# A two-layer attention and long-convolution kernel: skip row by identity products, closing tiles in another pool, two groups of loads reordered

## The chip, the cores and the metric

The kernel runs on 1 core of one Trainium2 chip. The metric is the device time of an execution in microseconds (us). In the text the engines are PE (TensorE), DVE (VectorE), ACT (ScalarE), POOL (GpSimd) and SP (SyncE, which here issues nearly all transfers). L524 is line 524 of the kernel before; in the kernel after, the same statements stand at a line one to ten away.

## The reference

Inputs are 2048 latent tokens and 256 context tokens of width 1024, in fp32. Layer 0 has global attention (8 query heads, 2 key heads of width 64) beside a Hyena long convolution of order 2; layer 1 has windowed attention with a sink beside two-dimensional neighbourhood attention. The branches are gated, joined by an output projection, and added to the residual. What the change touches in the convolution: the filter taps of each order are divided by their norm, and the convolved signal gets the input times `skip` added.

```python
def bidir_long_conv(z, h_fwd, h_bwd, d_skip):
    n = z.shape[1]
    taps = jnp.concatenate([h_fwd, jnp.zeros_like(h_fwd[:1]), h_bwd[:0:-1]], axis=0)
    taps = taps * lax.rsqrt(jnp.sum(taps * taps, axis=0, keepdims=True) + EPS)
    zf = jnp.fft.rfft(z.astype(jnp.float32), n=2 * n, axis=1)
    tf = jnp.fft.rfft(taps, n=2 * n, axis=0)
    y = jnp.fft.irfft(zf * tf[None], n=2 * n, axis=1)[:, :n]
    return (y + z.astype(jnp.float32) * d_skip.astype(jnp.float32)).astype(z.dtype)
...
def hyena_branch(u, conv_w, conv_b, w1, b1, w2, b2, freq, w3, d_skip):
...
    for o in range(HYENA_ORDER):
        z = parts[o + 1] * bidir_long_conv(z, filt[:, o, 0], filt[:, o, 1], d_skip[o])
...
def even_mixer(p, p_ctx, q_norm, k_norm, conv_w, conv_b, w1, b1, w2, b2, freq, w3, d_skip, cos, sin, need_ctx):
...
    y_a = global_gqa(q, k, v, k_c, v_c)
    y_b = hyena_branch(hu, conv_w, conv_b, w1, b1, w2, b2, freq, w3, d_skip)
    y = jnp.concatenate([y_a * jax.nn.silu(ag), y_b * jax.nn.silu(hg)], axis=-1)
```

In each layer the mixer's output `y` goes through `x = x + gate[:, None] * jnp.matmul(y, w_out[layer])`. The kernel puts `d_skip` into the filter: adding `d_skip * sqrt(sum of squares + EPS)` to tap 0 ahead of the division by the norm is the same as adding `z * d_skip` to the convolution's result.

## The kernel before, in words

All of it is one core's program. Matrix products of fp32 data are made of three products of high and low parts (`mm3`, L222: `whi` by high, `whi` by low, `wlo` by high part). A weight tile of 256 KB is loaded by SP into a ring of three `wraw` tiles (L242), cast to `whi` by ACT (L243), and POOL makes `wlo` (L244).

Every engine takes its instructions in order. Which order that is, a list scheduler decides for each engine at build time, with modelled durations; only PE's order in the two attention stages is written by hand. So an edit to one stage can reorder the instructions of all engines around it. SP's queue matters most here: a DMA that must wait for its data or for its target's buffer holds up all DMAs behind it. Memory comes from pools that are opened and closed by stage; a pool that takes the memory of a closed one waits for that one's last users.

The stages in order of time: conditioning and the first loads (0 to 60 us); the filters of the Hyena convolution between layer-0 projections (to 600); context attention and context Hyena (to 790); projections, latent convolution and the first maxima (to 1174); global attention in 16 units, with Hyena steps and jobs of the output projection between (1190 to 2303); layer-1 projections of three groups of tokens (2303 to 2510, to 2800, to 3128); layer-1 attention (to 3720); the last output projection.

The parts that the change and the prediction touch:

- `filter_loads` (L405 to L446) lists the loads of the filters' constants; `filters` computes. `taps` (L486 to L531) is run for the context filters (twice, one round for each order `o`, near 115 to 150 us) and for the latent filters (near 560 to 600 us). In each round, four matmuls sum the squares of the taps into `pss` (L519), with the channel on the partitions (128x4); DVE adds EPS (L521), ACT and DVE make the reciprocal root `rc` (L118 to L124), and DVE multiplies to the norm `ssv` (L523). The first tap row `first[o]` has its 512 channels along one partition, so the norm must change its layout: SP stores it to HBM (`rD`, L524, single elements), reads it back as 1x512 (`ssq`, L526), loads the skip row (`dskip`, L528), and DVE multiplies and adds (L529, L530). Then `behind` casts the tap tile (L456) and transforms it (`pA`, L562).
- `finish` in `glob_attn` closes a unit of the attention: it loads the gate `agt`, sums the denominators (`pd`, L1003), copies them (`rec`, L1005), takes reciprocals in four quarters (L1008, DVE), multiplies by gate and values (L1011, L1012, POOL), and `finish_y` splits the result into `yhi` and `ylo` (L370, L371) and stores both to `yT` (L372, L373). All these tiles come from the attention's pool `ga`. Behind the last unit, the normalised input of layer 1 (`lnh`, L306, then `hT`, L307 and L308) and the gains of the norms (L273, scaled at L275) take memory of the closed `ga`.
- `out_jobs` makes the jobs of the output projection; `job` loads weights and two `oy` tiles (L1390) of a token tile and calls `mm3`. Pool `xo` holds its rings: `oy0` and `oy1` of two tiles each, 4 KB a partition.
- In each group of layer 1, `rows` and `cols` of `Proj` project: keys and values of the window, its queries, the neighbourhood's keys, queries and values (`ev_v`, tile `vt`, store `v1n`, L353), then the gates in two blocks of `cols`. The stores of queries and keys are `qk<-tq` (L215). In the last group `window_keys` (L1429 to L1444) loads mask, sink, banded keys `wk1` and `wk2` (L1441, L1442) and values (L1443) of layer 1's windowed attention, which first uses them at L1550.

Of the kernel before, what the change touches and what calls it, by code (L numbers as in the profile page):

```python
# [17 lines left out]
P = 128  # L18
# [22 lines left out]
def kern(ctx, tc, nc, I, C, out):  # L41
# [114 lines left out]
    fC = dr.tile([2, 4, P, 512], F32, tag="fC", name="fC")  # L156
    rD = dr.tile([4, 512], F32, tag="rD", name="rD")
    q0 = [dr.tile([8, P, min(512, 2304 - t)], F32, tag=f"q0{t}", name="q0") for t in range(0, 2304, 512)]
# [91 lines left out]
    class Proj:  # L250
# [98 lines left out]
        def ev_v(self, dst):  # L349
            def f(ps, tt):  # L350
                vt = self.rg.tile([P, 512], F32, tag="bo", name="vt", bufs=3)
                S.copy(vt, ps)
                nc.sync.dma_start(dst[tt], vt)  # L353
            return f
# [10 lines left out]

    def finish_y(sb, y, ft, t0, n, yT=yT, tags=("yhi", "ylo"), bufs=2, eng=None):

        hi = sb.tile([P, 512], F32R, tag=tags[0], name="yhi", bufs=bufs)
        lo = sb.tile([P, 512], F32R, tag=tags[1], name="ylo", bufs=bufs)
        S.copy(hi[:, :n], y)  # L370
        (eng or V).tensor_tensor(out=lo[:, :n], in0=y, in1=hi[:, :n].bitcast(F32), op=ALU.subtract)  # L371
        nc.sync.dma_start(yT[0, ft, :, t0:t0 + n], hi[:, :n].bitcast(F32))  # L372
        nc.sync.dma_start(yT[1, ft, :, t0:t0 + n], lo[:, :n].bitcast(F32))  # L373
# [12 lines left out]
    def scr(sb, nm):  # L386
        return sb.tile([P, 512], F32, tag="s", name=nm, bufs=SC)
# [17 lines left out]
    def filter_loads(sb, ztiles):  # L405
# [38 lines left out]
        D["dA"] = t = scr(sb, "dA")[:, 0:P]  # L444
        ld.append(lambda t=t: nc.sync.dma_start(t, C['dftAf']))
        return D, ld  # L446

    rc = [cp.tile([P, 2, 4], F32, tag=f"rc{i}", name=f"rc{i}") for i in range(2)]

    def filters(sb, ps, D):  # L450
        zf, w1, pc, w2, dl, dscc, w3, dsc, dA = (D[k] for k in ("zf", "w1", "pc", "w2", "dl", "dscc", "w3", "dsc", "dA"))
        def new(nm, *shape, tag=None, bufs=1, dt=F32R):
# [33 lines left out]
        def taps(nq, mm, dcol, behind, ctxt):  # L486
# [29 lines left out]
            for o in range(2):  # L516
                pt = ps.tile([P, 512], F32, tag="x", name="pss", bufs=3)
                for k in range(4):
                    T.matmul(pt[:, k:k + 1], acc[o][:, k * P:(k + 1) * P], ones[:, 0:1], start=True, stop=True)  # L519
                v = sb.tile([P, 4], F32, tag="ssv", name="ssv", bufs=2)  # L520
                V.tensor_scalar(out=v, in0=pt[:, 0:4], scalar1=EPS, scalar2=None, op0=ALU.add)  # L521
                rsqrt(sb, rc[ctxt][:, o, :], v, 4, "sst")
                V.tensor_tensor(out=v, in0=v, in1=rc[ctxt][:, o, :], op=ALU.mult)  # L523
                nc.sync.dma_start(rD[2 * ctxt + o].rearrange("(k p) -> p k", p=P), v)  # L524
                v = scr(sb, "ssq")[0:1]
                nc.sync.dma_start(v, rD[2 * ctxt + o:2 * ctxt + o + 1])  # L526
                ds_ = scr(sb, "dskip")[0:1]
                nc.sync.dma_start(ds_, I['hy_skip'][0, o:o + 1, :])  # L528
                V.tensor_tensor(out=v, in0=v, in1=ds_, op=ALU.mult)  # L529
                V.tensor_tensor(out=first[o][0:1, :], in0=first[o][0:1, :], in1=v, op=ALU.add)  # L530
                behind(o, 0, first[o])()  # L531
# [370 lines left out]

    def glob_attn(sb, ps, hooks, M0):

# [91 lines left out]
        def finish(n, yo, acc):  # L996

            qb, hp = units[n]
            gt = sb.tile([P, 512], F32, tag="agt", name="agt", bufs=1)
            nc.sync.dma_start(gt, g0[hp, :, qb * 512:qb * 512 + 512])  # L1000
            pd = ps.tile([P, 512], F32, tag="m", name="pd", bufs=3)
            for h in range(2):
                T.matmul(pd[64 * h:64 * h + 64, :], ones[:, 64:P], acc[:, h, :], start=True, stop=True)  # L1003
            rec = sb.tile([P, 512], F32, tag="rec", name="rec", bufs=1)
            S.copy(rec, pd)  # L1005

            def quarter(i):
                V.reciprocal(rec[:, i:i + 128], rec[:, i:i + 128])  # L1008

            def gate():  # L1010
                G.tensor_tensor(out=rec, in0=rec, in1=gt, op=ALU.mult)  # L1011
                G.tensor_tensor(out=yo, in0=yo, in1=rec, op=ALU.mult)  # L1012

            return [lambda i=i: quarter(i) for i in range(0, 512, 128)] + [gate, lambda: finish_y(sb, yo, hp, qb * 512, 512, bufs=1, eng=G)]

        batches = [(n, kt) for n in range(16) for kt in range(0, 18, 2)]
        nb = len(batches)
        acc, po, ended, last, pend = {}, {}, {}, None, []
        total = 16 * 41

# [8 lines left out]
        for b in range(nb + 4):  # L1029
# [23 lines left out]
            if last is not None:  # L1053
                m, ks, tiles = last
                if ks == 0:
                    po[m] = ps.tile([P, 512], F32, tag="o", name="po", bufs=1)
                for i in range(2):
                    values(m, ks + i, tiles[i], po[m])
                if ks == 16:
                    yo = sb.tile([P, 512], F32, tag="yo", name="yo", bufs=2)  # L1060
                    S.copy(yo, po.pop(m))
                    ended[b + 2] = m, yo
# [307 lines left out]
    def out_jobs(g, halves, xs=None, early=()):  # L1370
# [9 lines left out]
        def job(b, i, tt, mm):  # L1380
            c = slice(512 * b, 512 * b + 512)
            rg, xo, gl = O0["rg"], O0["xo"], O0["gl"]
            if i == 0 and w_out.get("b") != b:
                w_out["b"] = b
                w_out["w"] = load_w(I['w_out'][0][:, c], 512)
            if g == 0 and i == 0:
                gate_half(gl[:, c], mm("pg"), 0, 0, b)
            ty = [xo.tile([P, 8, P], F32R, tag=f"oy{s}", name=f"oy{s}", bufs=2) for s in range(2)]
            for s in range(2):
                nc.sync.dma_start(ty[s].bitcast(F32), yT[s, :, :, tt * P:(tt + 1) * P].rearrange("f p t -> p f t"))  # L1390
            gate = gl[:, c]
# [36 lines left out]

    def window_keys():  # L1429

# [6 lines left out]
        wk2 = aw.tile([P, 2304], F32R, tag="wk2", name="wk2")  # L1437
        wvt = aw.tile([P, 18, P], F32, tag="wv", name="wv")
        for s in range(2):
            r = slice(64 * s, 64 * s + 64)  # L1440
# [9 lines left out]
    def hooks(b):  # L1450
# [9 lines left out]
        return [], [], []  # L1460

    HB, PB = 2, 5
    with tc.manual_schedule(engines={mybir.EngineType.PE}):
        glob_attn(ga, gap, hooks, M0)
    for j in jobs:
# [16 lines left out]
    for g in range(3):  # L1482
# [14 lines left out]
        pj.rows(0, 512, False, pj.ev_q(lambda tt: qk1[0:8][:, :, tt * P:(tt + 1) * P], 'win_q_norm', -0.125, True))  # L1497
        if g == 2:
            wm, sk, wk1, wk2, wvt = window_keys()
        pj.rows(1280, 512, True, pj.ev_q(lambda tt: qk1[18:26][:, :, tt * P:(tt + 1) * P], 'nat_k_norm', 1.0, False))  # L1500
        pj.rows(768, 512, False, pj.ev_q(lambda tt: qk1[10:18][:, :, tt * P:(tt + 1) * P], 'nat_q_norm', -0.125, False))
        pj.rows(1792, 512, True, pj.ev_v(v1n))
        for b in range(2):
            pj.cols(2304 + 512 * b, True, g1[4 * b:4 * b + 4], False)
# [462 lines left out]
```

## Time and profile before

| what | before |
|---|---|
| median of three runs | 3899.59 us (3898.86, 3899.59, 3904.81) |
| the profiled execution | 3905.59 us |
| its span | 3903.8 us |
| busy PE | 3627.0 us, 93% of the span |
| busy DVE, ACT, POOL | 59%, 46%, 44% |
| mean granted clock of PE | 0.97 |
| bytes moved by DMA | 586 MB, 150 GB/s |

How to read the lines that the prediction shows. A row of a timeline has the start, the duration, the engine, the line, the operation and its tiles (out<-in) and, in brackets, how long the engine stood idle before and whose end released it. A row of a window has its bounds and length, then the busy time of PE, of PE's weight loads, of DVE, ACT and POOL (with the number of instructions), then the granted clock of PE (1 is full speed), the busy share of the DMA engines and GB/s. A row of waits has the waiting engine and line, the releaser, and total us, count and longest.

### The profile page before, as it was taken

The numbers are of one execution on the slowest core, as the hardware profiler recorded it, in microseconds if no ns is written. First come the engines' busy times: TensorE is split into PE (matmuls) and PEld (weight loads), VectorE is DVE, ScalarE is ACT, GpSimd is POOL, SyncE is SP. The second block draws the span as 40 slices with busy tenths as digits, with TensorE's granted clock in tenths as the row PEclk, the third lists the DMA queues.
The fourth block names the chain that finished last, engine by engine and source line by source line (L and its number), as shares of the span: only waits on it lengthen the run. The fifth ranks groups of instructions, "written<-read, shape, count | busy, mean of one in ns | idle before, by whom it ended". The sixth has DMA issues, their size and how long they took to land.

```text
span 3903.8 us, 57140 instructions
## 1 busy us (share of the span) xinstructions
PE 3627.0 (93%) x20080; PEld 2615.3 (67%) x20080; DVE 2305.7 (59%) x4370; ACT 1802.8 (46%) x3482; POOL 1733.5 (44%) x1433
## 2 busy tenths in 40 slices
PE   6799989997788999999998989999998999999999
PEld 2588767756574554455545657887876878888887
DVE  6754762626877775677664338286158267677622
ACT  4554652413535665566453334344233266666610
POOL 1444552213245786767797555353244222132310
PEclk9899999999898999999999999999999999999999
DMA  6444344465567555343343454555465375365355
GB/s 197 93 135 132 134 119 119 135 215 191 164 182 221 172 163 185 119 144 117 108 161 112 135 159 139 168 168 152 139 191 160 118 180 139 91 161 133 112 175 168
DMA packets 536337, 586.23 MB, mean 150 GB/s; under 512 B 71318, under 2 KB 362448, under 8 KB 531954
## 3 DMA queue, kind: packets, MB, share of 16 engines
q1 hardware_dynamic: 519778, 551.12, 48.5%
q10 hardware_dynamic: 13856, 25.18, 1.7%
q0 software_dynamic: 2416, 6.29, 0.6%
q8 instruction: 158, 2.59, 0.3%
q14 instruction: 129, 1.06, 0.1%
HBM read 389.63 MB, written 192.76 MB: 149 GB/s over the span
## 4 chain that ended last, share of the span: by engine, by line
PE 59%; DVE 8%; DMA 5%; issue 5%; ACT 3%; POOL 2%; SPq 0%; ACTq 0%; POOLq 0%; DVEq 0%
PE psB L222 8%; PE pso L222 7%; PE psA L222 6%; PE po L994 6%; PE npt L1569 4%; PE no L1581 4%; PE pS L975 4%; PE pm L888 3%; PE pS L976 3%; PE ns L1550 2%; PE ns L1556 2%; PE hpX L802 1%; PE hpC L795 1%; PE hpH L807 1%; DMA wraw<-in_w_in_dram 1%
## 5 line engine op out<-in xcount | busy, mean ns | idle before, releaser
L244 POOL TENSOR_TENSOR wlo<-wraw,whi 128x512 fp32r<-128x512 f32 x368 | 500.9, 1376 | 832.8 <-ACT whi L243 657.5
L989 POOL TENSOR_TENSOR pacc<-pacc,Pt 128x512 f32<-128x512 f32 x512 | 646.0, 1284 | 193.1 <-ACT Pt L977 191.4
L222 PE MATMUL psB<-hT,whi 128*128 128x512 f32 (+1 forms) x2560 | 667.1, 350 | 29.5 <-DVE u L714 8.9
L222 PE MATMUL psA<-whi,hT 128*128 128x512 f32 (+1 forms) x1952 | 571.3, 373 | 34.1 <-DVE u L717 11.3
L222 PEld LDWEIGHTS psB<-hT,whi 128*128 128x128 f32 x2560 | 451.9, 193 | 107.6 <-issue 13.1
L889 DVE TENSOR_REDUCE mx<-pm 128x1 f32<-128x512 f32 (+1 forms) x640 | 389.6, 631 | 185.5 <-PE pm L888 181.3
L977 ACT ACTIVATE Pt<-pS 128x512 f32<-128x512 f32 x576 | 332.9, 597 | 351.8 <-PE pS L976 326.1
L222 PE MATMUL psB<-hT,wlo 128*128 128x512 f32 (+1 forms) x1280 | 442.2, 351 | 8.0 <-POOL wlo L244 7.8
L222 PEld LDWEIGHTS psA<-whi,hT 128*128 128x128 f32 x1952 | 356.8, 193 | 103.5 <-DVE u L717 11.5
L243 ACT CAST whi<-wraw 128x512 fp32r<-128x512 f32 x368 | 222.0, 618 | 312.3 <-DMA wraw<-in_w_in_dram 141.4
L222 PE MATMUL psA<-wlo,hT 128*128 128x512 f32 (+1 forms) x976 | 356.6, 370 | 0.8 <-POOL wlo L244 0.5
L222 PE MATMUL pso<-whi,oy 128*128 128x512 f32 x1088 | 344.2, 395 | 9.1 <-DMA oy<-yT 8.2
L975 PE MATMUL pS<-Q,K 128*128 128x512 f32 x576 | 331.2, 575 | 10.2 <-ACT Pt L977 9.5
L994 PE MATMUL po<-Pt,V 128*64 128x512 f32 x1152 | 287.2, 621 | 0.0
L222 PEld LDWEIGHTS psB<-hT,wlo 128*128 128x128 f32 x1280 | 245.9, 193 | 46.8 <-POOL wlo L244 12.1
L1569 PE MATMUL npt<-ident,np 128*128 128x128 f32 x1488 | 258.2, 283 | 3.3 <-DVE ggt L1153 1.9
L975 PEld LDWEIGHTS pS<-Q,K 128*128 128x128 f32 x576 | 110.1, 191 | 205.2 <-issue 99.8
L222 PEld LDWEIGHTS pso<-whi,oy 128*128 128x128 f32 x1088 | 205.9, 190 | 60.4 <-issue 7.6
L976 PE MATMUL pS<-Q,K 65*128 65x512 f32 x576 | 231.9, 403 | 5.8 <-DMA Q<-mr 5.8
L888 PE MATMUL pm<-K,Q 128*128 128x512 f32 x600 | 217.3, 384 | 17.3 <-DVE mx L889 16.0
L222 PE MATMUL pso<-wlo,oy 128*128 128x512 f32 x544 | 213.7, 395 | 1.2 <-POOL wlo L244 1.2
L222 PEld LDWEIGHTS psA<-wlo,hT 128*128 128x128 f32 x976 | 188.8, 194 | 31.4 <-POOL wlo L244 2.4
(342 smaller groups left out, 6500.4 us busy)
## 6 DMA issues: line engine op xcount, KB each, us to landing
wraw<-in_w_in_dram SPq DMA_DIRECT2D x312, 256.0 KB
oy<-yT SPq DMA_DIRECT2D x72, 512.0 KB
qk<-tq SPq DMA_DIRECT2D x50, 512.0 KB
fA<-fev SPq DMA_DIRECT2D x64, 256.0 KB
hxb<-XA SPq DMA_DIRECT2D x64, 256.0 KB
hfb<-fA SPq DMA_DIRECT2D x64, 256.0 KB
XC<-hevc ACTq DMA_DIRECT2D x64, 256.0 KB
hdi<-XC SPq DMA_DIRECT2D x64, 256.0 KB
```

What stands on the lines that cost most here:

```text
L222: T.matmul(ps, a(x, kt), b(y, kt), start=(kt == 0 and n == 0), stop=(kt == 7 and n == 2))
L243: S.copy(hi, w)
L244: G.tensor_tensor(out=lo, in0=w, in1=hi.bitcast(F32), op=ALU.subtract)
L888: T.matmul(pm[:, :n], self.q1[:, h, qt * P:(qt + 1) * P], self.K1(c0, n), start=True, stop=True)
L889: V.tensor_reduce(out=self.mx[:, u, c:c + 1], in_=pm[:, :n], axis=AX.X, op=ALU.max)
L975: T.matmul(s, K1[kv][:, kt * P:(kt + 1) * P], q1[:, h, :], start=True, stop=False)
L976: T.matmul(s, K2[kv][:, kt * P:(kt + 1) * P], q2[:, h, :], start=False, stop=True)
L977: S.activation(pt[:, h, :], s, AF.Exp)
L989: G.tensor_tensor(out=acc[1][:, h], in0=acc[1][:, h], in1=p[:, h], op=ALU.add)
L994: T.matmul(po[64 * h:64 * h + 64, :], vt[:, kt, kv * 64:kv * 64 + 64], p[:, h, :], start=(kt == 0), stop=(kt == 17))
L1569: T.transpose(pt[:, i, :], self.p[h][:, (i0 + i) * P:(i0 + i + 1) * P], ident)
L1581: T.matmul(B["po"][64 * h:64 * h + 64, self.k, :], vt[:, kt, 64 * h:64 * h + 64], self.pT[h, i // 4][:, i % 4, :], start=(i == 0), stop=(i ...
```

## The change

Four things change.

1. The skip row. Two loads at the start bring `hy_skip` with the channel on the partitions (`skip`, 128x2x4, one load of 128x4 single elements for each order). In `taps`, DVE multiplies the norm by it there (128x4), and four matmuls with one column of that as the stationary operand and the identity as the moving one lay it out as a row 1x512 in PSUM (`pskip`, ring of three shared with `ptap` and `pss`); DVE adds it from there. The tensor `rD`, its stores, the reads of it and the loads of the skip row (12 DMAs) are gone; 16 matmuls are new.
2. The closing tiles of the last attention unit (gate, denominators, values, `yhi`, `ylo`) are halves of three tiles from the rings `oy0` and `oy1` of the pool `xo` and no longer tiles of `ga`.
3. `window_keys` is called after the neighbourhood's values, and three one-column copies by DVE from the last `vt` tile into the targets hold its big loads until that tile is there.
4. `job` issues its two `oy` loads ahead of the weights and the gate.

```diff
+        t = new("skip", P, 2, 4)
+        add("skip", t, *[(t[:, o], I['hy_skip'][0, o].rearrange("(k p) -> p k", p=P)) for o in range(2)])
...
                 V.tensor_tensor(out=v, in0=v, in1=rc[ctxt][:, o, :], op=ALU.mult)
-                nc.sync.dma_start(rD[2 * ctxt + o].rearrange("(k p) -> p k", p=P), v)
-                v = scr(sb, "ssq")[0:1]
-                nc.sync.dma_start(v, rD[2 * ctxt + o:2 * ctxt + o + 1])
-                ds_ = scr(sb, "dskip")[0:1]
-                nc.sync.dma_start(ds_, I['hy_skip'][0, o:o + 1, :])
-                V.tensor_tensor(out=v, in0=v, in1=ds_, op=ALU.mult)
-                V.tensor_tensor(out=first[o][0:1, :], in0=first[o][0:1, :], in1=v, op=ALU.add)
+                V.tensor_tensor(out=v, in0=v, in1=skip[:, o], op=ALU.mult)
+                pt = ps.tile([P, 512], F32, tag="x", name="pskip", bufs=3)
+                for k in range(4):
+                    T.matmul(pt[0:1, k * P:(k + 1) * P], v[:, k:k + 1], ident, start=True, stop=True)
+                V.tensor_tensor(out=first[o][0:1, :], in0=first[o][0:1, :], in1=pt[0:1, :], op=ALU.add)
                 behind(o, 0, first[o])()
...
-            gt = sb.tile([P, 512], F32, tag="agt", name="agt", bufs=1)
+            tail = iter(home[0]) if n == 15 else None
+            gt = next(tail) if tail else sb.tile([P, 512], F32, tag="agt", name="agt", bufs=1)
...
-            rec = sb.tile([P, 512], F32, tag="rec", name="rec", bufs=1)
+            rec = next(tail) if tail else sb.tile([P, 512], F32, tag="rec", name="rec", bufs=1)
...
-                    yo = sb.tile([P, 512], F32, tag="yo", name="yo", bufs=2)
+                    if m == 15:
+                        home[:] = last_home()
+                    yo = home[0].pop() if m == 15 else sb.tile([P, 512], F32, tag="yo", name="yo", bufs=2)
...
+            ty = [xo.tile([P, 8, P], F32R, tag=f"oy{s}", name=f"oy{s}", bufs=2) for s in range(2)]
+            for s in range(2):
+                nc.sync.dma_start(ty[s].bitcast(F32), yT[s, :, :, tt * P:(tt + 1) * P].rearrange("f p t -> p f t"))
             if i == 0 and w_out.get("b") != b:
...
-            ty = [xo.tile([P, 8, P], F32R, tag=f"oy{s}", name=f"oy{s}", bufs=2) for s in range(2)]
-            for s in range(2):
-                nc.sync.dma_start(ty[s].bitcast(F32), yT[s, :, :, tt * P:(tt + 1) * P].rearrange("f p t -> p f t"))
...
+        for t in (wk1[:, 0, 0:1], wk2[:, 0:1], wvt[:, 0, 0:1]):
+            V.tensor_copy(t, late[:, 0:1])
...
+    def last_home():
+
+        ty = [O0["xo"].tile([P, 8, P], (F32, F32, F32R)[i], tag=f"oy{i % 2}", name="yl", bufs=2).rearrange("p a b -> p (a b)") for i in range(3)]
+        return [ty[0][:, :512], ty[0][:, 512:], ty[1][:, :512]], (ty[2][:, :512], ty[2][:, 512:])
...
-        if g == 2:
-            wm, sk, wk1, wk2, wvt = window_keys()
...
         pj.rows(1792, 512, True, pj.ev_v(v1n))
+        if g == 2:
+            wm, sk, wk1, wk2, wvt = window_keys(pj.late)
```

What this does to the order of the engines is shown at three places. The first is the context filters. On SP the stores and reads of the norm stood between loads of weights (`wraw`) and stores of the projection (`v`, `k`, `fC`); before:

```order
L363 DMA v_87<-vt 128x128
L524 DMA rD<-ssv 128x4x1
L242 DMA wraw<-in_w_in_dram 128x512
L526 DMA ssq<-rD 1x512
L528 DMA dskip<-in_hy_skip_dram 1x512
L524 DMA rD<-ssv 128x4x1
L215 DMA k_86<-tq_2326 128x2x128
L242 DMA wraw<-in_w_in_dram 128x512
L526 DMA ssq<-rD 1x512
L572 DMA fC<-tap 128x512
L528 DMA dskip<-in_hy_skip_dram 1x512
```

They are gone from SP. On PE the products take a place of their own; `pt` are transposes, `psA` matmuls of the projection; after:

```order
L221 MATMUL psA<-wlo,hT_1988 128x512
L528 MATMUL pskip<-ident,ssv 1x128 x4
L520 MATMUL pss<-ones,acc_395 128x1 x4
L208 MATMUL pt_2386<-ident,qn_2379 128x128
L208 MATMUL pt_2439<-ident,qn_2436 128x128
L221 MATMUL psA<-whi,hT_1989 128x512
```

The first round's sums stand 37 rows ahead of the first row shown, the second round's sums directly behind the first round's products, the second round's products 34 rows further on, and the first transform `pA` 27 rows behind those. Before, the two rounds' sums stood eight rows apart.

The second place is the end of global attention on DVE, where the reciprocals of the last unit are followed by layer 1's `hT` and the scaling of two gains; before:

```order
L1008 RECIPROCAL rec<-rec 128x128 x4
L307 CAST hT_19964<-lnh 128x512
L308 TENSOR_TENSOR hT_19965<-lnh,hT_19964 128x512
L307 CAST hT_19964<-lnh 128x512
L275 TENSOR_SCALAR gwin_q_norm<-gwin_q_norm 128x64
```

And after (`yl` is a closing tile in its new home):

```order
L1008 RECIPROCAL yl<-yl 128x128 x4
L274 TENSOR_SCALAR gwin_q_norm<-gwin_q_norm 128x64
L306 CAST hT_19964<-lnh 128x512
L274 TENSOR_SCALAR gnat_q_norm<-gnat_q_norm 128x64
L306 CAST hT_19964<-lnh 128x512
```

The scaling of the gains has moved ahead of the casts.

The third place is SP in the last group of layer 1. Before, the banded keys stand among the stores of queries and keys:

```order
L215 DMA qk_96<-tq_25419 128x2x128
L1443 DMA wv<-v1w 128x18x128
L215 DMA qk_96<-tq_25476 128x2x128
...
L1441 DMA wk_26053<-qk_96 64x2x2304
L1442 DMA wk_26054<-qk_96 64x2304
L1441 DMA wk_26053<-qk_96 64x2x2304
L1442 DMA wk_26054<-qk_96 64x2304
L215 DMA qk_96<-tq_25752 128x8x128
```

After, they stand behind the last store of the neighbourhood's values and ahead of weights and stores of the gates (`g`):

```order
L241 DMA wraw<-in_w_in_dram 128x512 x3
L352 DMA v1n<-vt 128x512
L1446 DMA wk_27001<-qk_95 64x2x2304
L1447 DMA wk_27002<-qk_95 64x2304
L1446 DMA wk_27001<-qk_95 64x2x2304
L1447 DMA wk_27002<-qk_95 64x2304
L1448 DMA wv<-v1w 128x18x128
L241 DMA wraw<-in_w_in_dram 128x512 x3
L342 DMA g_98<-bo 128x512 x2
L241 DMA wraw<-in_w_in_dram 128x512 x2
```

All five big loads have moved past the second projection of the group, its stores and its weights.

More of the change, by code (lines that the diff above doesn't have):

```diff
@@ L156, in kern @@
     fC = dr.tile([2, 4, P, 512], F32, tag="fC", name="fC")
-    rD = dr.tile([4, 512], F32, tag="rD", name="rD")
     q0 = [dr.tile([8, P, min(512, 2304 - t)], F32, tag=f"q0{t}", name="q0") for t in range(0, 2304, 512)]
@@ L350, in f @@
             def f(ps, tt):
-                vt = self.rg.tile([P, 512], F32, tag="bo", name="vt", bufs=3)
+                vt = self.late = self.rg.tile([P, 512], F32, tag="bo", name="vt", bufs=3)
                 S.copy(vt, ps)
@@ L364, in ev_kv, with finish_y @@
             return f
-    def finish_y(sb, y, ft, t0, n, yT=yT, tags=("yhi", "ylo"), bufs=2, eng=None):
-        hi = sb.tile([P, 512], F32R, tag=tags[0], name="yhi", bufs=bufs)
-        lo = sb.tile([P, 512], F32R, tag=tags[1], name="ylo", bufs=bufs)
+    def finish_y(sb, y, ft, t0, n, yT=yT, tags=("yhi", "ylo"), bufs=2, eng=None, home=None):
+        hi = home[0] if home else sb.tile([P, 512], F32R, tag=tags[0], name="yhi", bufs=bufs)
+        lo = home[1] if home else sb.tile([P, 512], F32R, tag=tags[1], name="ylo", bufs=bufs)
         S.copy(hi[:, :n], y)
@@ L450, in filters @@
     def filters(sb, ps, D):
-        zf, w1, pc, w2, dl, dscc, w3, dsc, dA = (D[k] for k in ("zf", "w1", "pc", "w2", "dl", "dscc", "w3", "dsc", "dA"))
+        zf, w1, pc, w2, dl, dscc, w3, dsc, dA, skip = (D[k] for k in ("zf", "w1", "pc", "w2", "dl", "dscc", "w3", "dsc", "dA", "skip"))
         def new(nm, *shape, tag=None, bufs=1, dt=F32R):
@@ L901, in first_maxima, with glob_attn @@
         return Maxima(lambda c, n: ks[c // 1024][:, c % 1024:c % 1024 + n], q1, mx, bank)
-    def glob_attn(sb, ps, hooks, M0):
+    def glob_attn(sb, ps, hooks, M0, last_home):
         K1, K2 = [None] * 2, [None] * 2
@@ L1012, in gate @@
                 G.tensor_tensor(out=yo, in0=yo, in1=rec, op=ALU.mult)
-            return [lambda i=i: quarter(i) for i in range(0, 512, 128)] + [gate, lambda: finish_y(sb, yo, hp, qb * 512, 512, bufs=1, eng=G)]
+            return [lambda i=i: quarter(i) for i in range(0, 512, 128)] + [gate, lambda: finish_y(sb, yo, hp, qb * 512, 512, bufs=1, eng=G, home=home[1] if tail else None)]
         batches = [(n, kt) for n in range(16) for kt in range(0, 18, 2)]
@@ L1018, in glob_attn @@
         acc, po, ended, last, pend = {}, {}, {}, None, []
+        home = []
         total = 16 * 41
@@ L1427, in residual, with window_keys @@
             i += nt
-    def window_keys():
+    def window_keys(late):
         wm = aw.tile([P, 1152], F32, tag="wm", name="wm")
@@ L1460, in hooks @@
         return [], [], []
+    def last_home():
+        ty = [O0["xo"].tile([P, 8, P], (F32, F32, F32R)[i], tag=f"oy{i % 2}", name="yl", bufs=2).rearrange("p a b -> p (a b)") for i in range(3)]
+        return [ty[0][:, :512], ty[0][:, 512:], ty[1][:, :512]], (ty[2][:, :512], ty[2][:, 512:])
     HB, PB = 2, 5
     with tc.manual_schedule(engines={mybir.EngineType.PE}):
-        glob_attn(ga, gap, hooks, M0)
+        glob_attn(ga, gap, hooks, M0, last_home)
     for j in jobs:
```

## The prediction

> **What bounds the kernel now.** I read the page first: the span and the busy times.
>
> ```profile
> span 3903.8 us, 57140 instructions
> PE 3627.0 (93%) x20080; PEld 2615.3 (67%) x20080; DVE 2305.7 (59%) x4370; ACT 1802.8 (46%) x3482; POOL 1733.5 (44%) x1433
> ```
>
> TensorE (PE) is busy in 93% of the span: 3903.8 - 3627.0 = 277 us are left, spread over many stages. A change gains only where PE stands still, or where it runs at half its clock after standing still. So I read each edit's place in the table by windows, then the timelines around the holes and the waits that end them. The profiled execution took 3905.59 us, the median of the runs is 3899.59; the sum is a difference, and I take it off the median (off the profiled execution it gives 6 us more).
>
> **The change part by part: the skip row, context filters.** Next, the waits of SP's queue over the span (total, times, longest), the instructions of two tiles (durations in ns, first and last start), timelines of SP, VectorE (DVE) and PE, and windows (PE busy is the first column after the length, the granted clock stands behind the five engines).
>
> ```profile
> SPq L526 <- DMA rD<-ssv: 35.1, 4, 9.9
> L519 PE MATMUL pss<-ones,acc x32: 168/250/353, 114.4 to 581.9; 128*128 128x1 f32 x32
> L523 DVE TENSOR_TENSOR ssv<-ssv,rc x4: 161/162/164, 122.8 to 586.0; 128x4 f32<-128x4 f32 x4
> 123.07 0.39 SPq L524 DMA_DIRECT2D rD<-ssv  x1
> 133.95 0.24 SPq L526 DMA_DIRECT2D ssq<-rD  x1
> 135.78 0.68 DVE L529 TENSOR_TENSOR ssq<-ssq,dskip 1x512 f32<-1x512 f32 x1 [8.26 <-DMA dskip<-in_hy_skip_dram]
> 147.83 0.80 PE L562 MATMUL pA<-st,dAh 128*128 128x512 f32 x1 [4.48 <-ACT st L456]
> 125.00:130.00 5.00, 5.00 (x24) 4.03 (x23) 2.15 (x8) 0.57 (x3) 1.30 (x1) 1.00 0.57 23
> 130.00:150.00 20.00, 5.29 (x15) 3.52 (x14) 5.39 (x13) 5.06 (x10) 0.00 (x0) 0.61 0.49 62
> 150.00:155.00 5.00, 5.00 (x20) 3.97 (x20) 4.71 (x16) 2.76 (x6) 0.13 (x1) 0.85 0.23 79
> ```
>
> The row is stored to HBM at 123.07 and read back only at 133.95, since SP waits at L526 until the store has landed. DVE works through one in-order queue: L529 waits for that row, and the evacuations behind it, which PE needs, wait with it. PE idles 20 - 5.29 = 14.7 us from 130 to 150. Its clock in there is 0.61 in the mean. The work after the first hole, about 4.3 of the 5.29 us, ran at half clock, which is 2.2 us lost, and from 150 to 155 another 0.15 x 5 = 0.75. The hole is worth 17.6 us if nothing is late in its place.
>
> Something is. The sums of squares must still go through the rsqrt chain to `v`, and now PE multiplies `v` before DVE can add. In the new order some 38 matmuls lie between the sums (`pss`) and the products (`pskip`), at 24 in 5 us about 38 x 0.21 = 8 us. The chain takes 122.8 - 114.4 = 8.4 us (first starts of the two tiles), so it is just covered. The second round's sums now stand behind the first round's products, and 26 matmuls lie between the last product and the transform that needs it. I take -15, between -11 (the 10.9 us between store and read) and -17.6.
>
> A rule of the Trainium skill ("TensorE: Matmul & The Clock Gate", section "What's actually happening") says that the clock comes back to full after one busy window of about 3.4 us. By it one hole without the short resumption in its middle would cost 3.4 / 2 = 1.7 us of slow clock; the rows above hold 2.2 + 0.75 = 2.95, so the sum by the page would be 1 us smaller, and the rows decide.
>
> **The skip row, latent filters.** SP's timeline, PE's, and windows:
>
> ```profile
> 572.50 0.24 SPq L526 DMA_DIRECT2D ssq<-rD  x1
> 574.00 9.49 SPq L242 DMA_DIRECT2D wraw<-in_w_in_dram  x6
> 575.64 1.22 PE L222 MATMUL psB<-hT,whi 128*128 128x512 f32 x2 [4.03 <-ACT whi L243]
> 570.00:605.00 35.00, 27.42 (x93) 21.32 (x92) 9.81 (x19) 6.07 (x11) 6.29 (x5) 0.76 0.34 94
> 575.00:585.00 10.00, 9.23 (x25) 7.17 (x26) 4.64 (x7) 4.83 (x9) 5.96 (x5) 0.50 0.51 139
> 600.00:605.00 5.00, 5.00 (x13) 3.92 (x12) 0.57 (x2) 0.58 (x1) 0.00 (x0) 0.50 0.14 52
> ```
>
> The victim here is the weight stream behind the wait on SP: the next weights are issued after 572.50, and PE waits 4.03 us for the cast of one. The idle time from 570 to 605 is 35 - 27.42 = 7.6 us. At a clock of 0.50 stand 9.23 + 5.00 us of work, half of which, 7.1, is lost. Together 14.7. I take -14, from -8 (the idle time alone) to -15. What is late next: PE has matmuls of the projection to run, 34 to 41 of them between sums and products.
>
> **What the products cost.** Sixteen 1x128 matmuls on 128 columns of ident. The trace has no such shape; next to it stand the sums (`pss`, above: one column moved) and the transposes by ident (128x128 moved):
>
> ```profile
> 2315.50 1.11 PE L303 MATMUL lnpt<-ident,ox 128*128 128x128 f32 x4 [9.93 <-ACT lnh L306]
> ```
>
> The sums' 16 instructions left 32 records, so an instruction of plain fp32 is two. Lower end 16 x 0.168 = 2.7 us (the records overlap), upper end 32 x 1.11 / 4 = 8.9. The transposes move as many columns, at one record each 4.4; I take +5. What DVE saves (a 1x512 product of 0.68 us becomes a 128x4 one) is beside PE's work: nothing.
>
> **Two new loads at the start.** `skip` comes in two loads of 128x4 single elements, ahead of two `adaw` loads on SP, and PE waits for `adaw`. Rows: the queue's packets and share, and PE at such a wait.
>
> ```profile
> q1 hardware_dynamic: 519778, 551.12, 48.5%
> 48.35 4.43 PE L95 MATMUL ada<-adaw,sil 128*32 128x512 f32 x16 [3.67 <-DMA adaw<-in_w_ada_dram]
> ```
>
> A packet takes 0.485 x 3903.8 x 16 / 519778 = 0.058 us of one engine in the mean, so 1024 elements as packets of their own take at most 1024 x 0.058 / 16 = 3.7 us of all 16, at the least nothing that PE sees. I take +2.
>
> Against this part speaks a rule of the Trainium skill ("DMA: Bandwidth & Descriptors", section "Rules for kernel authors"): a strided last dimension becomes one descriptor per element. By it the price goes with the 1024 elements and not with the 4 KB; the upper end above would hold, and the sum would be 1.7 us worse.
>
> **The last unit's closing tiles.** Timelines of DVE, SP, ACT and PE where layer 1 begins:
>
> ```profile
> 2304.44 3.39 DVE L1008 RECIPROCAL rec<-rec 128x128 f32<-128x128 f32 x4 [10.98 <-ACT rec L1005]
> 2312.57 0.32 SPq L373 DMA_DIRECT2D yT<-ylo  x1
> 2315.99 0.42 SPq L273 DMA_DIRECT2D gwin_q_norm<-in_win_q_norm_dram  x1
> 2319.96 0.67 DVE L275 TENSOR_SCALAR gwin_q_norm<-gwin_q_norm 128x64 f32<-128x64 f32 x1 [2.99 <-DMA gwin_q_norm<-in_win_q_norm_dram]
> 2314.67 1.44 ACT L306 ACTIVATE lnh<-lnpt,gs 128x512 f32<-128x512 f32 x2 [3.46 <-DMA yT<-ylo]
> 2316.26 0.56 PE L222 MATMUL psA<-whi,hT 128*128 128x256 f32 x1
> ```
>
> `lnh` takes memory of the attention's pool, so it waits until the last unit's `ylo` has been stored; PE idles 9.93 us. With the closing tiles elsewhere `lnh` needs only the attention itself to end. Next late is DVE: the four reciprocals end at 2307.8, and in the new order the scaling of a loaded gain stands between them and the first cast. That gain came 2319.96 - 2315.99 = 4 us after its issue; issued near 2304.5, once the attention's last matmuls free the memory, it is there near 2308.5. With the scaling, the cast and the subtraction of `hT` (three times some 0.67) the first psA comes near 2310.5 instead of 2316.26. So -6, from -3 (gains later by 3) to -9.
>
> **The banded keys held back.** The loads with their sizes, two pieces of the chain, windows, and timelines of SP and PE:
>
> ```profile
> wk<-qk SPq DMA_DIRECT2D x2, 1152.0 KB
> wk<-qk SPq DMA_DIRECT2D x2, 576.0 KB
> 2937.28 16.65 DMA qk<-tq
> 2978.59 3.69 DMA qk<-tq
> 2935.00:2960.00 25.00, 15.85 (x62) 11.74 (x63) 17.90 (x28) 8.31 (x17) 14.89 (x12) 0.88 0.94 223
> 2960.00:3035.00 75.00, 72.63 (x338) 58.52 (x337) 66.86 (x136) 32.49 (x67) 27.90 (x22) 1.00 0.51 149
> 3062.74 0.33 SPq L353 DMA_DIRECT2D v1n<-vt  x1
> 3061.00:3128.00 67.00, 67.00 (x383) 58.52 (x382) 7.69 (x14) 14.71 (x26) 12.99 (x11) 1.00 0.32 101
> 3130.17 0.74 PE L1550 MATMUL ns<-wk,wq 128*128 128x256 f32 x4 [1.48 <-DVE bo L340]
> ```
>
> Behind the keys a store takes 16.65 us that elsewhere takes 3.69; DVE needs its buffer. PE idles 25 - 15.85 = 9.15 us from 2935 to 2960, plus some 2 us of slow clock. Afterwards DVE is at 66.86 of 75 us, so it can take up most but not all: -8, from -4 to -11. Held back, the loads start behind the last `v1n` store. The keys are 2 x 1152 + 2 x 576 = 3456 KB, the values 18 x 128 x 128 x 4 bytes = 1152 KB: 4608 KB at 223 GB/s are 21 us, so they land by about 3085, hidden by gate columns in which PE is busy 67 of 67 us, and are first used at 3130.17. Five weights of the second gate block stand behind them on SP; PE needs those from about 3095, the middle of the 67 us, since the two blocks are equal work. Give-back: +1, from 0 to 5. The three DVE copies that hold the loads stand behind the last `vt` copy, before anything else needs DVE: nothing.
>
> **Operands of the out projection first.** The new order on SP differs from the old only at the job group that begins near 2030 (in the groups of layer 1 those operands were already ahead). There:
>
> ```profile
> 2000.00:2100.00 100.00, 87.27 (x323) 44.61 (x322) 54.12 (x83) 45.01 (x81) 94.42 (x78) 0.91 0.50 166
> ```
>
> POOL is busy 94.42 of 100 us, the same work stands in the same order, so an `oy` that comes sooner waits for the weights instead: 0, from -2 to +2.
>
> **The order from 900 to 1174.** The scheduler writes this stretch anew. Windows, and two of PE's waits there:
>
> ```profile
> 900.00:1174.00 274.00, 216.89 (x1090) 170.31 (x1089) 211.02 (x315) 122.38 (x196) 99.95 (x86) 0.89 0.57 176
> PE hpA L669 <- DVE zst L381: 12.1, 1, 12.1
> PE psA L222 <- DVE u L717: 11.3, 1, 11.3
> ```
>
> PE idles 57 us here; the same work in another order may lose or win a wait of this size. No row gives a sign: 0, from -10 to +10, one such wait.
>
> **The sum:** -15 - 14 + 5 + 2 - 6 - 8 + 1 + 0 + 0 = -35, so 3899.6 - 35 = 3864.6 us, said as 3864.
>
> **The rivals.** First, only the round trips pay: the closing tiles and the keys merely move a wait (to the gains, to DVE), -35 + 6 + 8 - 1 = -22, so 3878. For it speaks that DVE is next in both places; against it that a store of 16.65 us vanishes and PE is at 72.63 of 75 us right behind. Second, the products eat the gain of the filters: should PE reach `pskip` before `v` is there, it stops in its own queue, at worst for the 8.4 us of the sums' chain in each of four rounds, 34 of the 35, so 3898; if only the two first rounds stop, 3881. Against it speak the 34 to 41 matmuls between. Third, on the other side: the new order from 900 to 1174 leaves PE idle twice as long, +57 - 35 = +22, so 3922; it decides from 43 us more on. For it: DVE is at 211 of 274 us and PE's waits there are single long ones that hang on order. Against it: two waits of the largest size make only 24. That the change does not do what it says I leave out: the twelve DMAs are gone from SP's order and the keys stand behind `v1n`.
>
> **How the numbers follow.** My forecast 0.58, the first rival 0.24, the second 0.09, the third 0.05, better than all terms' good ends 0.04. The bounds of the terms lie 2.6, 1, 2.3, 2, 3, 3, 1, 2 and 10 us on the good side of the values taken, and 4, 6, 3.9, 1.7, 3, 4, 4, 2 and 10 on the bad side; as they are independent, I add them by squares: 12 and 15, so the forecast's own range is 3852 to 3880. On the bad side the range reaches past the first rival to where one of its terms is bad as well, 3885, on the good side to a little more than all good ends but the reorder's (17), 3846. About 0.2% (8 us) is what a measurement of this kernel can tell from no change. Faster by more: the forecast, the first rival, the good end and 0.03 of the second, 0.89. Within it: 0.06 of the second and 0.01 of the third, 0.07. Slower: the rest of the third, 0.04.
>
> **What would show it.** Right: no DMA between L519 and the add, PE nearly full from 125 to 155 and 570 to 605 at a clock near 1; `lnh` at about 2305 in old time; no store above 6 us in the second projection of the last group; PE full through the gate columns. Wrong: PE waits at `pskip` for DVE, psB waits for `wlo` in the second gate block, or more idle time from 900 to 1174 than 57 us.

## The result and the profile after

The changed kernel takes 3857.42 us in the median (3855.33 to 3859.86) against 3899.23 us before (3895.39 to 3904.81): a ratio of 0.9892, 95% interval 0.9875 to 0.9909, which is 42 us, between 35 and 49. Measured again beside three other kernels, with its own runs of before, it was 3858.02 us, 0.9902 (0.9888 to 0.9915), 38 us. The forecast was 3864 us, 35 less, with a range from 3846 to 3885. The profiled executions differ by more than the medians (3905.6 against 3857.3), because the one of before was 6 us above its median.

The page of the changed kernel; PE's work is the same but for the products (3631.9 us busy, 3627.0 before), the span is 48 us shorter:

```profile
span 3855.5 us, 57187 instructions
PE 3631.9 (94%) x20112; PEld 2613.5 (68%) x20112; DVE 2290.8 (59%) x4373; ACT 1800.5 (47%) x3480; POOL 1732.8 (45%) x1433
```

**The filters.** The first products of context attention (`gs`) come behind all filters in either kernel. Here are their rows in the profile of before and then of after; the number to read is the start, ahead of "to":

```profile
L1093 PE MATMUL gs<-ck,cq x16: 276/280/390, 617.9 to 664.5; 128*128 128x256 f32 x16
```

```profile
L1096 PE MATMUL gs<-ck,cq x16: 276/279/386, 589.9 to 636.9; 128*128 128x256 f32 x16
```

They start 28 us sooner. The windows of after that answer to the holes of before (130 to 150, and the latent filters), the products, and the transform that waited before:

```profile
130.00:150.00 20.00, 20.00 (x102) 15.68 (x101) 17.19 (x55) 8.01 (x21) 9.09 (x7) 1.00 0.33 100
550.00:580.00 30.00, 30.00 (x163) 24.82 (x163) 8.74 (x22) 5.62 (x10) 6.79 (x5) 1.00 0.40 124
130.58 1.03 PE L528 MATMUL pskip<-ident,ssv 128*1 128x128 f32 x8
147.48 0.40 PE L561 MATMUL pA<-st,dAh 128*128 128x512 f32 x1
```

PE is busy for all of 20 and all of 30 us at a clock of 1.00, where it had 5.29 of 20 at 0.61. No idle time stands ahead of `pskip` or `pA`. Four products are 1.03 us of PE, 4.1 for all sixteen.

**From 900 to 1174.** The same stretch, 28 us earlier, of the new order:

```profile
872.00:1147.00 275.00, 226.73 (x1073) 175.45 (x1071) 212.31 (x323) 121.88 (x194) 96.41 (x87) 0.85 0.57 175
```

PE stands still for 48 us in place of 57, but at a clock of 0.85 in place of 0.89. Measured from the first `gs` to the first scores of global attention, the stretch lasts 562.6 us before and 561.2 after: the new order neither won nor lost.

**The start of layer 1.** Timelines of DVE, SP, ACT and PE after:

```profile
2274.47 3.39 DVE L1008 RECIPROCAL yl<-yl 128x128 f32<-128x128 f32 x4 [10.56 <-ACT yl L1005]
2276.59 6.99 SPq L241 DMA_DIRECT2D wraw<-in_w_in_dram  x4
2279.42 0.61 DVE L274 TENSOR_SCALAR gwin_q_norm<-gwin_q_norm 128x64 f32<-128x64 f32 x1 [1.57 <-DMA gwin_q_norm<-in_win_q_norm_dram]
2275.89 1.45 ACT L305 ACTIVATE lnh<-lnpt,gs 128x512 f32<-128x512 f32 x2
2280.42 0.38 PE L221 MATMUL psA<-whi,hT 128*128 128x256 f32 x1 [2.38 <-DVE hT L306]
```

From the reciprocals on, `lnh` comes 1.4 us later in place of 10.2, and the first psA 5.95 us later in place of 11.82. What is late now is the gain, as forecast: DVE waits 1.57 us for it, and PE 2.38 for the cast behind it. The four weights of the second row went out 2.1 us behind the reciprocals. Before, SP issued them 13.7 us behind them, since the stores of `yT` and the loads of the gains stood ahead:

```profile
2318.14 8.78 SPq L242 DMA_DIRECT2D wraw<-in_w_in_dram  x4
```

**The banded keys.** The window where the hole was, SP and PE after:

```profile
2895.00:2920.00 25.00, 23.91 (x104) 18.19 (x103) 22.95 (x36) 11.27 (x23) 21.09 (x16) 1.00 0.56 159
3012.00:3080.00 68.00, 67.15 (x384) 58.49 (x383) 7.97 (x17) 14.30 (x26) 12.77 (x10) 1.00 0.63 168
3013.85 0.61 SPq L1446 DMA_DIRECT2D wk<-qk  x1
3017.79 17.52 SPq L241 DMA_DIRECT2D wraw<-in_w_in_dram  x3
3082.01 0.74 PE L1560 MATMUL ns<-wk,wq 128*128 128x256 f32 x4 [1.50 <-DVE bo L339]
```

PE is busy 23.91 of 25 us there, against 15.85. The loads run beside the gate columns, where the DMA share has gone from 0.32 to 0.63 and PE has lost 0.85 us. The three weights behind the keys occupy SP for 17.52 us, but PE waits for no weight there; its one wait, 0.9 us, is for DVE.

### The profile page after: what moved, and what is told of

Its sections match the earlier page's. It is cut to its first block, busy times and chain, and to the rows that moved or that the text cites. A ratio compares the mean times of both kernels' runs of the same rounds, so it can differ in the third digit from the quotient of the medians.

```text
span 3855.5 us, 57187 instructions
## 1 busy us (share of the span) xinstructions
PE 3631.9 (94%) x20112; PEld 2613.5 (68%) x20112; DVE 2290.8 (59%) x4373; ACT 1800.5 (47%) x3480; POOL 1732.8 (45%) x1433
## 4 chain that ended last, share of the span: by engine, by line
PE 64%; DVE 15%; issue 6%; DMA 6%; ACT 5%; POOL 3%; SPq 1%; ACTq 0%; DVEq 0%; POOLq 0%; another core or an unknown queue 0%
PE psB L221 13%; PE pso L221 7%; PE po L993 6%; PE npt L1579 5%; PE psA L221 4%; PE no L1591 4%; PE pS L974 4%; PE pm L887 3%; PE pS L975 3%; PE ns L1560 2%; PE ns L1566 2%; DVE tq L213 1%; PE hpX L801 1%; DMA wraw<-in_w_in_dram 1%; PE hpC L794 1%
## 5 line engine op out<-in xcount | busy, mean ns | idle before, releaser
L221 PEld LDWEIGHTS psB<-hT,whi 128*128 128x128 f32 x2560 | 449.0, 192 | 92.3 <-issue 10.9
L221 PEld LDWEIGHTS psA<-whi,hT 128*128 128x128 f32 x1952 | 357.5, 193 | 93.7 <-ACT vt L361 13.7
```

Of the source, the lines that this page charges most:

```text
L221: T.matmul(ps, a(x, kt), b(y, kt), start=(kt == 0 and n == 0), stop=(kt == 7 and n == 2))
```

## The experiments

The first four kernels are the kernel before with one part each; the diff of each is that part of the change. The comparison is with runs of before on the same chip.

**Part 1 alone, the skip row.**

> The kernel before with part 1 of the change alone (skip row by identity products, two loads at the start). Theory, by the drift of the two profiles (first products of context attention 617.9 before, 589.9 after): 28 us faster, PE full from 130 to 150, and no idle time of 10 us at the transposes of k there. Rival (the order of the rest is what pays, the round trips were only half of it): 15 us or less.

3879.98 us, ratio 0.9961 (0.9949 to 0.9973): 15 us faster, 11 to 20 (13 by the medians). Its profiled execution (3871.2 us) was the shortest of its six, and has `gs` at 587.6:

```profile
L1092 PE MATMUL gs<-ck,cq x16: 276/279/384, 587.6 to 632.9; 128*128 128x256 f32 x16
```

The hole at the transposes is gone. The measured time is nearer to the rival, the profile to the theory; the reverse of it, below, was made to decide.

**Part 2 alone, the closing tiles.**

> The kernel before with part 2 alone (the last unit's closing tiles in the out projection's pool). Theory: the first psA of layer 1 comes 6 us sooner behind the last pd, and the run is 6 to 8 us faster. Rival (the weights and gains are what layer 1 waits for, the wait only moves to them): 2 us or less, with PE idle by the same sum from 2300 to 2400.

3884.48 us, 0.9971 (0.9959 to 0.9983): 11 us faster, 7 to 16. That is above the theory's 6 to 8, though the interval does not shut 8 out, which is also the difference of the medians. The first 25 us behind the last `pd`, in the profile of before and then of this kernel:

```profile
2303.00:2328.00 25.00, 12.43 (x86) 11.42 (x86) 10.92 (x18) 9.32 (x15) 10.85 (x9) 0.80 0.23 72
```

```profile
2291.50:2316.50 25.00, 20.48 (x141) 18.64 (x138) 20.80 (x25) 12.80 (x22) 17.31 (x12) 0.86 0.63 194
```

PE works 8 us more in this window, not 6: the weights (DMA 194 in place of 72 GB/s) and the next normalisations come sooner as well. How much each of the two is worth was not separated. The rival is out.

**Part 3 alone, the banded keys.**

> The kernel before with part 3 alone (banded keys held back). Theory: the store of 16.65 us at 2937 shrinks to about 4, PE's idle time there of 9 us goes, 8 us faster, of which about 1 is given back in the gate columns. Rival (VectorE bounds the second projection of the group, so the hole is only spread): 3 us or less.

3889.26 us, 0.9988 (0.9979 to 0.9996): 5 us faster, 2 to 8. The window of the hole and the gate columns:

```profile
2922.00:2947.00 25.00, 23.80 (x104) 18.00 (x104) 22.85 (x38) 11.18 (x24) 20.47 (x17) 1.00 0.54 150
3041.00:3108.00 67.00, 65.61 (x372) 57.02 (x371) 7.97 (x17) 14.23 (x26) 12.75 (x10) 1.00 0.62 167
```

The hole is closed, and the gate columns give back 1.4 us. What PE waited for in the hole can be followed by two rows of before, and by ACT's waits for the buffers of these stores, summed from the load of the mask to the end of the neighbourhood's values (total, times, longest), before and then here:

```profile
2953.95 0.58 ACT L213 CAST tq<-pt 64x512 fp32r<-64x512 f32 x1 [10.54 <-DMA qk<-tq]
2956.78 1.22 PE L222 MATMUL psA<-whi,hT 128*128 128x512 f32 x2 [7.28 <-ACT whi L243]
ACT tq L213 <- DMA qk<-tq: 18.3, 6, 10.5
ACT tq L213 <- DMA qk<-tq: 1.7, 3, 0.7
```

It was ACT that stood still for the buffer of the slow store, 10.54 us, and the casts of the weights behind it in ACT's order kept PE waiting for 7.28. DVE, which the prediction names, waited for ACT. From the load of the mask to the first use of the keys it is 227.2 us here, 233.2 before: 6 us. The eight other profiles that hold this part have 225.8 to 227.6, the four others without it 231.7 to 233.1, so of the four parts this one is measured best.

**Part 4 alone, the out projection's operands.**

> The kernel before with part 4 alone (the out projection's operands loaded ahead of its weights). Theory: no change, within 2 us, since POOL bounds the place where the order differs. Rival (the profiles' drift of 5 us between the first psA of layer 1 and the last group's norm is this part's): 3 to 5 us faster.

3891.11 us, 0.9995 (0.9987 to 1.0004): no difference that can be told, as the theory said, though the interval reaches to 5 us faster. The profiles speak against the rival: from the last `pd` to the load of the mask it is 591.7 us with part 4 alone and 597.8 with all but part 2, against 594.1 to 597.5 in the four profiles with neither part. With part 2 alone it is 586.4, so most of the drift comes with part 2.

The four ratios multiplied give 0.9915. Next came the whole change again, part 1 from its other side, and two tests of single elements in transfers.

**The whole change again.**

> The changed kernel once more, as the base for the runs beside it and for a second profile. The first four parts alone measured 0.9961, 0.9971, 0.9988 and 0.9995 of the kernel before, together 0.9915; the whole change measured 0.9892. If the parts add up, the whole stands at about 0.990 to 0.9915 here; rival (the parts help each other): 0.989 or less.

3858.02 us, 0.9902 (0.9888 to 0.9915): the parts add up, within what the intervals can tell.

**All but part 1.**

> The changed kernel with part 1 undone (the norms go through HBM again). Theory, by the starts of the attention in the profiles so far (1169.7 to 1180.5 with the trip, 1149.8 and 1151.1 without): 24 us slower than the changed kernel. Rival (part 1 alone measured only 13 us, 0.9961): 13 us slower.

3875.31 us, 0.9951 (0.9938 to 0.9963), so part 1 is worth 17 us on top of the others by the medians, and by the two ratios some 12 to 26. Its `gs` start at 614.2:

```profile
L1097 PE MATMUL gs<-ck,cq x16: 276/279/388, 614.2 to 660.9; 128*128 128x256 f32 x16
```

The five profiles with the old trip have them between 607.6 and 617.9, mean 613.4; the two of the changed kernel, part 1 alone and all but part 2 have 587.6 to 589.9, mean 588.8. That is 24.6 us in the filters. PE's busy time up to there is alike in the nine, 524.5 to 531.8 us. Timed runs show 15 and 17 of them at the end. Less than 2 us are given back within global attention (from the first scores to the last `pd` 1116.9 us in the mean of the same five, 1118.5 of the four, which scatter by 6 to 11). Some 4 of the rest can lie in the executions that were profiled: those of the four kernels without the trip were 4.7 us below their kernels' medians in the mean, those of the five with it 0.5. With one profile of most kernels this stays open.

**The trip kept, its store in pieces of four elements.** Before, the 128x4 norm went to HBM as 512 single elements of 4 bytes. Here it is the kernel before with one line changed:

```diff
-nc.sync.dma_start(rD[2 * ctxt + o].rearrange("(k p) -> p k", p=P), v)
+nc.sync.dma_start(rD[2 * ctxt + o].rearrange("(p k) -> p k", p=P), v)
```

> The kernel before with the norm stored as 128 pieces of four elements in place of 512 single ones (the row that comes back holds the channels in another order, so the skip terms go to the wrong channels). Theory: the store's 10 us are the price of single elements, it lands some 5 us sooner in each of four rounds, and the run is 10 to 18 us faster than before. Rival: the 10 us are the way to HBM and the transfers queued ahead; no change within 4 us.

3876.76 us, 0.9952 (0.9939 to 0.9964): 19 us faster than before, as much as part 1. SP's timeline, the window of the hole, `gs`, and the packets of SP's queue:

```profile
122.13 0.38 SPq L524 DMA_DIRECT2D rD<-ssv  x1
122.61 0.38 SPq L242 DMA_DIRECT2D wraw<-in_w_in_dram  x1
124.52 0.24 SPq L526 DMA_DIRECT2D ssq<-rD  x1
130.00:150.00 20.00, 18.21 (x75) 13.16 (x76) 18.99 (x37) 12.07 (x21) 10.13 (x8) 1.00 0.23 76
L1093 PE MATMUL gs<-ck,cq x16: 274/279/384, 582.1 to 629.8; 128*128 128x256 f32 x16
q1 hardware_dynamic: 518242, 551.12, 48.4%
```

From store to read it is 2.4 us in place of 10.9, with a weight queued in between as before, and the hole is gone though the trip is still there. In the four rounds it is 1.8 to 3.2 us, against 8.3 to 10.9 in the profile of before. So the price was the 512 elements, not the way to HBM. This is the rule of the Trainium skill ("DMA: Bandwidth & Descriptors", section "Rules for kernel authors") that the prediction set against the new loads: a strided last dimension becomes one descriptor per element. The trace agrees: the queue moved 519778 packets before and 518242 here, 1536 fewer, which is 512 - 128 for each of the four stores. The rule bears on what the change removed more than on what it added.

The `gs` come 31 us sooner here than in the mean with the trip. PE was busy for only 519.4 us up to there, though, so some 9 us of that are work that now comes later.

**The skip values as eight rows, laid out at the start.** On the changed kernel:

```diff
-t = new("skip", P, 2, 4)
-add("skip", t, *[(t[:, o], I['hy_skip'][0, o].rearrange("(k p) -> p k", p=P)) for o in range(2)])
+t = new("skr", 8, P)
+add("skip", t, (t, I['hy_skip'][0].rearrange("o (k p) -> (o k) p", p=P)))
...
+pt = ps.tile([P, 512], F32, tag="x", name="pskr", bufs=3)
+T.matmul(pt[:, 0:8], skip, ident[0:8, 0:8], start=True, stop=True)
+skip = new("skip", P, 2, 4, dt=F32)
+V.tensor_copy(skip, pt[:, 0:8].rearrange("p (a b) -> p a b", b=4))
```

> The changed kernel with the skip values loaded as eight rows of 128 and laid on the partitions by one matmul with the identity and one copy. Theory: the two loads of single elements hold SP's queue for 3.1 us at 25.3 and all later weights of the conditioning come 3.2 us later, so this is 3 to 4 us faster than the changed kernel, with the first psA at about 68 to 70 in place of 72 to 74. Rival: the start is bound by the bytes of those weights, no change within 1.5 us.

3857.83 us, 0.9902 (0.9888 to 0.9917): no change, and the first psA at 73.5. But the experiment did not test what it was for, since PE now waited for the rows ahead of all filters:

```profile
PE pskr L461 <- DMA skr<-in_hy_skip_dram: 6.2, 1, 6.2
```

Its `gs` start at 607.6, 19 us later than the mean without the trip, and yet the time is the same. PE was busy for 538.9 us up to there, 526.3 and 527.6 in the two profiles of the changed kernel: about 12 us of the 19 are work that this kernel's order puts ahead of `gs`. From `gs` to the first scores it is then 552.5 us in place of 561.2 and 561.7. So the start of `gs` measures the filters only between kernels with like work ahead of it.

**The same, laid out only behind the first sums.** The four added lines of the last diff stand in `taps`, once, ahead of the first product by `skip`.

> The changed kernel with the skip values loaded as eight rows of 128, and laid on the partitions by one matmul and a copy only after the first sums of squares, not at the start. Theory (the loads of single elements delay the conditioning by 3 us, and the run with rows lost that again since PE waited 6.2 us for the rows at the start): first psA at 67 to 70, and 3 to 4 us faster than the changed kernel. Rival (what comes behind takes it up): no change within 1.5 us.

3848.14 us, 0.9879 (0.9862 to 0.9896), the fastest of all. SP's timeline in the changed kernel, and then in this one, with its `gs`:

```profile
25.30 3.10 SPq L411 DMA_DIRECT2D skip<-in_hy_skip_dram  x2
28.45 2.50 SPq L77 DMA_DIRECT2D adaw<-in_w_ada_dram  x2
```

```profile
25.20 0.62 SPq L411 DMA_DIRECT2D skr<-in_hy_skip_dram  x1
25.87 1.16 SPq L77 DMA_DIRECT2D adaw<-in_w_ada_dram  x2
L1102 PE MATMUL gs<-ck,cq x16: 274/279/385, 585.0 to 629.6; 128*128 128x256 f32 x16
```

The loads of single elements held SP for 3.10 us; rows hold it for 0.62. The first psA starts at 68.0, against 73.9 and 74.0 in the two profiles of the changed kernel, and `gs` 3.8 us sooner than the mean without the trip. So the start cost about 4 us, as the theory has it. The medians differ by 9 to 10, but their ratios' intervals overlap, and where more than 4 would come from is open.

**The products four times over.** `for k in (0, 1, 2, 3) * 4` in place of `for k in range(4)`.

> The changed kernel with each of the 16 products by the identity made four times over (the same result). Theory: 1.03 us of PE for four, all on the path since PE is full there, so 48 more cost 12 us. Rival (they fill gaps of PE): 4 us or less. A loss of 20 us or more would say that they also delay VectorE.

3866.28 us, 0.9925 (0.991 to 0.9941), between the theory and the rival. Their rows, and `gs`:

```profile
L528 PE MATMUL pskip<-ident,ssv x128: 270/272/273, 129.3 to 576.9; 128*1 128x128 f32 x128
L1096 PE MATMUL gs<-ck,cq x16: 274/279/386, 596.3 to 642.5; 128*128 128x256 f32 x16
```

Forty-eight more products cost 8 to 9 us, and `gs` is 7.5 later: sixteen cost 2.5 to 3, somewhat under their 4.1 us of PE. Most of them are on the path. Of the larger loss that would speak for DVE being held up there is no sign.

**All but part 2.**

> The changed kernel with part 2 undone (the last unit's closing tiles again in the attention's pool). Theory, by the profiles (from the last pd to the mask load of the last group 583 to 586 us with the part, 592 to 598 without): 10 to 11 us slower than the changed kernel, 4 of it in the normalisations and weights behind the first psA. Rival (only the first psA's 6 us were won): 6 us slower.

3868.56 us, 0.993 (0.9913 to 0.9946): 11 us slower than the changed kernel. By the two ratios alone it could be 3 to 19, so the times do not shut the rival's 6 out. PE's wait behind the last `pd`, and the 25 us from there, are nearly those of before:

```profile
2279.47 1.12 PE L302 MATMUL lnpt<-ident,ox 128*128 128x128 f32 x4 [10.15 <-ACT lnh L305]
2266.50:2291.50 25.00, 13.78 (x91) 12.74 (x89) 11.67 (x18) 9.34 (x15) 11.15 (x9) 0.73 0.24 75
```

**The trip with rows and the right channels.** Parts 2 to 4, and in place of part 1 a second set of sums, over the channels 4p+k, that can be stored in pieces of four:

```diff
+T.matmul(pt[:, k + 4:k + 5], acc[o].rearrange("c (p k) -> c k p", k=4)[:, k], ones[:, 0:1], start=True, stop=True)
...
+nc.sync.dma_start(rD[2 * ctxt + o].rearrange("(p k) -> p k", p=P), v[:, 4:8])
```

> Parts 2 to 4 of the change, and in place of part 1 the trip through HBM kept, with the norm summed a second time in an order that lets it be stored as 128 pieces of four elements and come back with the right channels (16 more matmuls of one column each, all results right). Theory (single elements were the price, not the trip): the store lands in about 2 us, and the run is as fast as the changed kernel, within 5 us, or faster. Rival (the trip itself costs, and the wrong order of the channels in the run before hid something): 10 us or more slower than the changed kernel.

3854.18 us, 0.9892 (0.9873 to 0.991): as fast as the changed kernel. The store and the read of the first round, and 120 to 150:

```profile
122.66 0.32 SPq L525 DMA_DIRECT2D rD<-ssv  x1
124.86 0.24 SPq L527 DMA_DIRECT2D ssq<-rD  x1
120.00:150.00 30.00, 30.00 (x131) 24.74 (x132) 23.54 (x71) 17.13 (x35) 12.46 (x11) 0.91 0.29 90
```

The way through HBM and the way through PE are worth the same here; the theory holds. The second of them includes the loads at the start, about 4 us, which this kernel does not have (its first psA starts at 68.4).

## Why the prediction was right, point by point

| term | forecast | measured |
|---|---|---|
| the two holes of the filters | -15 - 14 | -24.6 in all for part 1 at `gs`; less start and products about -31 |
| the products | +5 | +2.5 to +3 |
| the two loads at the start | +2 | about +4 |
| part 1 in all | -22 | -24.6 at `gs`; -15 and -17 at the end |
| closing tiles | -6 | -11 (alone), -11 (from the other side) |
| banded keys and give-back | -8 + 1 | -6 in the stretch; -5 at the end |
| operands first | 0 | -2, not to be told from 0 |
| the order from 900 to 1174 | 0 | -1 in the two profiles |

- **The holes.** The mechanism was as forecast, on DVE's and SP's queues both. One step was incomplete: the prediction took the store's 10.9 us as the price of the trip. The store in pieces of four shows that it is the price of 512 elements. The sum did not depend on it, since either way it goes.
- **The size of part 1.** The profile of before that the prediction stood on had larger holes than most: its `gs` at 617.9, the mean of five at 613.4. A hole that ends with the landing of 512 small pieces is not the same in every run: from store to read it is 7.6 to 11.0 us in the 20 rounds of the five profiles.
- **The products.** That an fp32 instruction is two records was right, the place in the order was right (PE never waited at `pskip`, so the second rival is out), the price was 2 us too high.
- **The loads at the start.** The upper end of 3.7 us was nearer than the 2 that were taken. Rows and a late layout took it away. It was priced by the time of mean packets; SP's 3.10 us at the issue is what was seen.
- **The closing tiles.** This step was mis-sized: it followed the first psA alone, and that was right (5.95 us behind the reciprocals, forecast 6.1). But the weights behind the `yT` stores on SP went out 11.6 us sooner and the second `lnh` was released as well, and PE's 25 us there held 8 us more work, at a higher clock. Measured 11 for 6; that the weights and the `lnh` make up the other 5 is argued from these rows, not measured by itself.
- **The keys.** The slow store was the cause of the hole, and its 9 us of idle time went, with a give-back near 1, as forecast. The step between was read wrongly: not DVE but ACT needed the store's buffer, and PE waited for the weights that ACT casts behind that. Of the 11 us of idle time and slow clock the forecast left 3 to DVE; the runs show 6 gained and 1 given back, and what took up the other 4 is not shown.
- **The reorder.** Ten us to either side were allowed, and 1 came. The third rival is out; that no row gave a sign was the right reading. The first rival (only the round trips pay) is out too, since parts 2 and 3 are both measured.

The 35 us of the forecast stand against 38 to 42, and part of the agreement is chance: part 1 gave less at the end than forecast, part 2 more.

## What to carry to other kernels

Before removing a small trip through HBM, look at the number of pieces it is cut into: a store of 512 single elements took 10.9 us where 128 pieces of 16 bytes took 2.4, and one changed line was worth as much as doing without the trip. When a wait at a stage boundary goes, follow what else stood behind it on the queue that issues the weights, not only the first instruction that starts sooner. Small loads that are put ahead of the first weights are paid at once; put them there as rows, and do what they need where nothing waits.

## What the runs showed of the hardware

- A 128x4 store of single elements holds the DMA engines at a high share for little data: from 130 to 150 us before, with such a store under way for most of it, a share of 0.49 moved 62 GB/s, and from 2960 to 3035 us a share of 0.51 moved 149 GB/s. With pieces of four both stores were over by 127 us, and from 130 to 150 a share of 0.23 moved 76 GB/s.
- Four such stores in pieces of four take 1536 packets fewer than in single elements (518242 against 519778 on SP's queue), as it must be with one packet for each piece.
- Two loads of 512 single elements keep SP's queue for 3.10 us at their issue, where the same values as eight rows take 0.62 us.
- A plain fp32 product 128x1 by 128x128 is two records of 272 ns that overlap: 1.03 us for four.
- The kernel before scatters: its runs lie between 3886.2 and 3904.8 us, and the starts of `gs` in the five profiles with the trips of before lie between 607.6 and 617.9, in the four with part 1 as it is in the change between 587.6 and 589.9.
